# One x load divided into four transfers, so that the sixteen DMA engines carry unequal shares

## The chip, the cores and the metric

The kernel runs on one core of one Trainium2 chip. The metric is device microseconds of one execution, the median of several runs. The profile is one further execution, recorded by the hardware profiler; its span runs from the program's first instruction to its last.

## What is computed

Eight experts, each with its own 256 tokens, two weight matrices and two biases:

```
h = np.matmul(x, w1) + b1[:, np.newaxis, :]
h = np.maximum(h, 0)
return (np.matmul(h, w2) + b2[:, np.newaxis, :]).astype(np.float32)
```

x is 8 x 256 x 512, w1 is 8 x 512 x 2048, w2 is 8 x 2048 x 512, and the output is 8 x 256 x 512, all fp32 in HBM. The kernel computes in fp16 with fp32 sums.

## The kernel before

**Loads.** Every load that GpSimd issues (the queue that the profile calls q0) converts fp32 in HBM to fp16 in SBUF on the way. `load_w1` (L82 to L86) and `load_w2` (L88 to L93) move one expert's matrix, 128 partitions with 16 KB of fp16 each; the w2 of the last two experts goes in two halves of 8 KB a partition. `load_x` (L72 to L80) moves the x of several experts in one transfer: experts 2 and 3 together (tile x2, 128 partitions with 4 KB of fp16 each, which are 8 KB in HBM) and experts 4 to 7 together. In x2, partition p holds four consecutive tokens; expert 2 lies in partitions 0 to 63, expert 3 in 64 to 127. The x of experts 0 and 1 comes as fp32 through SyncE's queue (L194, q1 in the profile) and is converted by VectorE. In what follows, a row is one partition's share of such a transfer.

**Order on the GpSimd queue.** The order is written out by hand in `ring` (L218 to L228): w1 of expert 0, b2, w1 of expert 1, the x2 load (L76), w1 of expert 2; then, each put ahead of a stage and issued when a buffer comes free, w1 of 3, w2 of 0, x of 4 to 7, w1 of 4, w2 of 1, and so on to the two halves of the w2 of expert 7. Three buffers for w1 and three for w2 let several 2 MB transfers stand in the queue at a time. Behind all loads, the same queue carries two stores (`flush`, L138 to L140): the results of experts 0 to 3, and those of 4 and 5.

**Work on each expert.** VectorE transposes x in 32x32 blocks (`transposes`, L96 to L112). `first_product` (L114 to L135) does 64 matmuls of 128x256 with a relu on ScalarE, and `second_product` (L166 to L186) 2 bias matmuls and 32 matmuls of 128x512, three stages later (LAG = 3). The results leave PSUM through VectorE and ScalarE in `store` (L142 to L164).

**The last stores.** The results of expert 6 leave in three parts, which SyncE (q1) and ScalarE (q10) issue, and those of expert 7 in one of 128 rows, which SyncE issues (L163, L164). A row is 4 KB here. The parts are set in

```
PARTS = {E - 2: ((0, 25, False), (25, 121, True), (121, 128, False))}
```

that is 25 rows on q1, 96 rows on q10, and 7 rows on q1.

**Landing.** Each transfer ends with sixteen small writes of 4 bytes, one of each DMA engine, that count up its semaphore; the engine that consumes the data waits until all sixteen are there. GpSimd's transfers take eight semaphores in turn.

Of the kernel before, what the change touches and what calls it, by code (L numbers as in the profile page):

```python
# [10 lines left out]
def kernel(  # L11
# [9 lines left out]
    nc = tc.nc  # L21
# [4 lines left out]
    P = 128  # L26
# [13 lines left out]
    PARTS = {E - 2: ((0, 25, False), (25, 121, True), (121, 128, False))}  # L40
    nXF32 = 2
    X_LOADS = {2: 2, 4: 4}

    def ordered(ins):
        return tc.keep_in_program_order(ins)
# [26 lines left out]
    def load_x(first, n):  # L72

        R = n * T // P
        t = x_pool.tile([P, R, H], fp16, tag=f"x{first}", name=f"x{first}")
        ordered(nc.gpsimd.dma_start(  # L76
            out=t, in_=x[first : first + n].rearrange("e (p r) h -> (e p) r h", r=R)
        ))
        for i in range(n):
            x16[first + i] = (t, i * (P // n), R)  # L80

# [110 lines left out]
    for e in range(nXF32):  # L192
# [4 lines left out]
        out=b2_sb,  # L197
        in_=b2.rearrange("e h -> (e h)").rearrange("(o f) -> o f", o=1),
    ))

    for e in range(nXF32):
        t = x_pool.tile([P, nTB, H], fp16, tag=f"x{e}", name=f"x{e}")
# [6 lines left out]
    for b in range(nB):  # L209
        nc.vector.transpose(  # L210
            out=b1T[b * B : (b + 1) * B, nB - 1 - b : nB - 1 - b + nJ * B],
            in_=b1_rows.rearrange("r (i j) -> r j i", j=nJ),
# [5 lines left out]
    for s in range(1, E + LAG - 1):  # L218
        if s < E:
            if s in X_LOADS:  # L220
                ring.append((s - 2, load_x, (s, X_LOADS[s])))
            ring.append((s - 2, load_w1, (s,)))
        if s >= LAG:
            ring.append((s - 2, load_w2, (s - LAG,)))
# [43 lines left out]
```

## Time and profile before

| | us |
|---|---|
| time, median of 3 runs (lowest, highest) | 181.61 (181.37, 181.66) |
| span of the profiled execution | 179.7 |
| time outside the span (median less span) | 1.9 |
| TensorE matmul busy | 130.7 |
| VectorE busy | 87.4 |
| ScalarE busy | 71.0 |
| GpSimd busy | 12.5 |

| queue | what it carries | packets | MB |
|---|---|---|---|
| q0 | GpSimd's loads and two stores | 3200 | 38.28 |
| q1 | SyncE's x loads and last stores | 476 | 1.70 |
| q10 | ScalarE's b1 load and a last store | 160 | 0.46 |
| q8, q14 | instruction fetch | 8 | 0.12 |

How to read it: an engine's busy time counts its own instructions alone. For the DMA engines the profile keeps every packet's queue, start, duration and size, but not which of the sixteen engines moved it, nor from which transfer it is. In a view of a window, the packets that start within it are counted by queue, with their bytes (as written at the destination) and the time that they took as a share of sixteen engines over the window. Packets under 512 bytes are nearly all the 4-byte landing marks, so their count in a window tells how many engines have come to the end of a transfer there.

### The profile page before, as it was taken

To read this page: it belongs to the slowest core of one execution; us is meant where nothing else is said; L and a number is where in the kernel's file an instruction comes from. 1 tells how busy PE (TensorE), PEld (TensorE's weight loads), DVE (VectorE), ACT (ScalarE), POOL (GpSimd) and SP (SyncE) were. 2 spreads that over 40 slices of the span, in tenths; PEclk is the share of its full clock that TensorE was granted. 3 is DMA by queue.
4 is the path that set the end of the run, shared out by engine and by line. 5 is a ranking of instruction groups with operands and counts; after the bars stand their busy time and mean duration, and the time that the engine had idled before them with its cause. 6 is when DMAs were issued, how large, how long until landed. Compare 5 with 4: busy or idle time off the path is not lost.

```text
span 179.7 us, 1958 instructions
## 1 busy us (share of the span) xinstructions
PE 130.7 (73%) x784; PEld 87.4 (49%) x784; DVE 87.4 (49%) x125; ACT 71.0 (40%) x152; POOL 12.5 (7%) x27
## 2 busy tenths in 40 slices
PE   0005999159895970999769994959499986999960
PEld 0004899149793320794359543934189432434420
DVE  0999938990000199999998699203200020301010
ACT  3001699318793022491267406930559020020010
POOL 6000030200201010001100001000200021010000
PEclk9999999858999696599988999999969997899998
DMA  5999999999998999999999999999999999999995
GB/s 208 274 197 213 233 204 208 230 224 193 228 233 184 224 233 219 193 230 230 193 219 233 212 197 233 230 193 219 233 208 201 233 212 202 217 215 213 344 422 239
DMA packets 3844, 40.56 MB, mean 226 GB/s; under 512 B 460, under 2 KB 476, under 8 KB 1148
## 3 DMA queue, kind: packets, MB, share of 16 engines
q0 software_dynamic: 3200, 38.28, 96.4%
q1 hardware_dynamic: 476, 1.70, 2.5%
q10 hardware_dynamic: 160, 0.46, 0.6%
q8 instruction: 6, 0.10, 0.2%
q14 instruction: 2, 0.02, 0.0%
HBM read 71.39 MB, written 4.19 MB: 421 GB/s over the span
## 4 chain that ended last, share of the span: by engine, by line
DMA 67%; PE 27%; POOL 1%; issue 1%; ACT 0%; another core or an unknown queue 0%; POOLq 0%
DMA w1sb<-in_w_dram 44%; DMA w2sb<-in_w_dram 23%; PE po L178 17%; PE ph L121 10%; PE po L171 1%; POOL w1sb L84 1%; ACT out L157 0%; POOL b_sb L196 0%; POOL x L76 0%; POOLq L252 0%
## 5 line engine op out<-in xcount | busy, mean ns | idle before, releaser
L121 PE MATMUL ph<-xT,w1sb 128*128 128x256 f16 x512 | 66.7, 299 | 36.2 <-DMA w1sb<-in_w_dram 30.0
L121 PEld LDWEIGHTS <-w1sb 128*128 128x128 f16 x512 | 60.9, 148 | 42.7 <-DMA w1sb<-in_w_dram 38.6
L128 ACT ACTIVATE hT<-ph,b1T 128x256 f16<-128x256 f32 x128 | 56.7, 475 | 36.9 <-PE ph L121 22.1
L112 DVE STREAM_TRANSPOSE xT<-x 32x256 f16<-32x256 f16 (+1 forms) x64 | 52.7, 885 | 28.0 <-DMA x<-in_x_dram 22.0
L178 PE MATMUL po<-w2sb,hT 128*128 128x512 f16 x256 | 59.9, 395 | 6.6 <-DMA w2sb<-in_w_dram 6.5
L178 PEld LDWEIGHTS <-hT 128*128 128x128 f16 x256 | 25.7, 101 | 40.7 <-issue 14.4
L156 DVE COPY out<-po 32x512 f32<-32x512 f32 (+2 forms) x22 | 15.1, 688 | 52.5 <-PE po L178 52.2
L157 ACT COPY out<-po 32x512 f32<-32x512 f32 (+2 forms) x22 | 12.7, 578 | 65.5 <-PE po L178 65.3
L109 DVE STREAM_TRANSPOSE xT<-x 32x256 f16<-32x256 f16 x32 | 14.0, 436 | 0.5
L93 POOL DMA_DIRECT2D w2sb<-in_w_dram x10 | 5.3, 535 | 73.9 <-PE po L178 73.9
L84 POOL DMA_DIRECT2D w1sb<-in_w_dram x8 | 4.5, 559 | 62.7 <-PE ph L121 61.9
L171 PE MATMUL po<-b_sb,ones 1*128 1x512 f16 x16 | 4.8, 379 | 0.0
L210 DVE STREAM_TRANSPOSE b1T<-b_rows 32x512 f32<-32x512 f32 x4 | 4.1, 1028 | 0.0
L203 DVE CAST x<-x 128x1024 f16<-128x1024 f32 x2 | 1.4, 694 | 3.3 <-DMA x<-in_x_dram 3.3
L171 PEld LDWEIGHTS <-ones 1*128 1x128 f16 x16 | 0.9, 92 | 2.1 <-issue 2.1
L140 POOL DMA_DIRECT2D out_dram<-out x2 | 1.1, 540 | 11.1 <-ACT out L157 11.1
L189 ACT ACT_TABLE_LOAD x1 | 1.3, 1283 | 0.7 <-PEq L252 0.7
L76 POOL DMA_DIRECT2D x<-in_x_dram x2 | 1.1, 557 | 0.0
L188 DVE MEMSET ones<- 1x128 f16 x1 | 0.2, 165 | 0.8 <-PEq L252 0.8
L196 POOL DMA_DIRECT2D b_sb<-in_b_dram x1 | 0.5, 507 | 0.0
L189 ACT ACTIVATE warm<-ones 1x128 f16<-1x128 f16 x1 | 0.3, 308 | 0.0
L252 POOL MEMSET const-float32-0.0<- 128x1 f32 x1 | 0.1, 98 | 0.2 <-issue 0.2
(3 smaller groups left out, 0.3 us busy)
## 6 DMA issues: line engine op xcount, KB each, us to landing
w1sb<-in_w_dram POOLq DMA_DIRECT2D x8, 2048.0 KB, 37.0
w2sb<-in_w_dram POOLq DMA_DIRECT2D x6, 2048.0 KB, 49.7
w2sb<-in_w_dram POOLq DMA_DIRECT2D x4, 1024.0 KB, 24.0
out_dram<-out POOLq DMA_DIRECT2D x1, 2048.0 KB, 26.7
x<-in_x_dram SPq DMA_DIRECT2D x2, 512.0 KB, 4.0
x<-in_x_dram POOLq DMA_DIRECT2D x1, 1024.0 KB, 35.6
out_dram<-out POOLq DMA_DIRECT2D x1, 1024.0 KB, 17.7
x<-in_x_dram POOLq DMA_DIRECT2D x1, 512.0 KB, 24.5
```

What stands on the lines that cost most here:

```text
L84: ordered(nc.gpsimd.dma_start(out=w1_sb[e], in_=w1[e].rearrange("(p kc) m -> p kc m", kc=nKC)))
L93: ordered(nc.gpsimd.dma_start(out=w2_sb[e][:, lo : lo + half], in_=src[:, lo : lo + half]))
L109: nc.vector.transpose(out=out[:, :, g, :, 0, :], in_=block[:, :, :, 0, :])
L112: nc.vector.transpose(out=out[:, tb, g], in_=block[:, tb])
L121: ordered(nc.tensor.matmul(out=ph, lhsT=w1_sb[e][:, kc, :].rearrange("p (q j) -> p q j", j=nJ)[:, :, j], rhs=xT[e][:, kc, :], start=(kc == 0),
L128: nc.scalar.activation(out=hT[e][:, j, :].rearrange("p (tb k i) -> p tb k i", tb=nTB, k=split), in_=ph.rearrange("p (tb i k) -> p tb k i", ...
L156: nc.vector.tensor_copy(out=out_sb[at : at + rows, k * nTB, :], in_=po[0][part])
L157: nc.scalar.copy(out=out_sb[at : at + rows, k * nTB + 1, :], in_=po[1][part])
L171: ordered(nc.tensor.matmul(out=t, lhsT=ones1, rhs=b2_sb[0:1, e * H : (e + 1) * H], start=True, stop=False,))
L178: ordered(nc.tensor.matmul(out=po[tb], lhsT=hT[e][:, j, tb * P : (tb + 1) * P], rhs=w2_sb[e][:, j, :], start=False, stop=(j == nJ - 1),))
L189: ordered(nc.scalar.activation(out=warm, in_=ones1, func=mybir.ActivationFunctionType.Relu))
L210: nc.vector.transpose(out=b1T[b * B : (b + 1) * B, nB - 1 - b : nB - 1 - b + nJ * B], in_=b1_rows.rearrange("r (i j) -> r j i", j=nJ),)
```

## The change

The load of x2 is issued as four transfers in place of one: rows 0 to 79, 80 to 101, 102 to 126, and 127. The second and the third carry `max_dma_last_dim` = 4096, which cuts each row of 8 KB in HBM into two descriptors of 4 KB (22x2x1024 and 25x2x1024 elements); the last row is divided into 16 pieces of 128 elements without being told. By the words of the change, eleven DMA engines then carry 7 rows and five carry 10; before, each carried 8. The four stand where the one stood in GpSimd's order.

```diff
     X_LOADS = {2: 2, 4: 4}
+    SHARES = {2: ((0, 80, None), (80, 102, 4096), (102, 127, 4096), (127, 128, None))}
...
         t = x_pool.tile([P, R, H], fp16, tag=f"x{first}", name=f"x{first}")
-        ordered(nc.gpsimd.dma_start(
-            out=t, in_=x[first : first + n].rearrange("e (p r) h -> (e p) r h", r=R)
-        ))
+        src = x[first : first + n].rearrange("e (p r) h -> (e p) (r h)", r=R)
+        dst = t.rearrange("p r h -> p (r h)")
+        for p0, p1, cap in SHARES.get(first, ((0, P, None),)):
+            ordered(nc.gpsimd.dma_start(
+                out=dst[p0:p1], in_=src[p0:p1], **({} if cap is None else {"max_dma_last_dim": cap}),
+            ))
```

Other loads go through the same lines as one transfer of 128 rows, as before. On the other engines the instructions stay as they are, in their order. GpSimd has three instructions more. Since the semaphores are taken in turn, each later transfer of GpSimd has another one, and the waits of the engines follow: VectorE's first 16 transposes of x2 (expert 2) wait for the 80 rows alone, the next 8 for the 22 rows too, and the last 8 for the 25 rows and the single one.

## The prediction

> **What bounds the kernel now.** I read the page first, for the resource that is always busy:
>
> ```profile
> span 179.7 us, 1958 instructions
> ...
> DMA  5999999999998999999999999999999999999995
> ...
> q0 software_dynamic: 3200, 38.28, 96.4%
> ...
> q8 instruction: 6, 0.10, 0.2%
> ```
>
> The sixteen DMA engines are busy from the second slice to the last but one, nearly all with GpSimd's queue. Then the chain of work that ended last, its last 70 us:
>
> ```profile
> 108.47 41.12 DMA w2sb<-in_w_dram
> 149.59 0.04 issue
> 149.63 8.75 PE po L178 x32
> ...
> 166.47 7.03 PE po L178 x32
> ...
> 173.52 0.59 ACT out L157
> ```
>
> The last w2 load that TensorE waits for was issued 41 us before it landed: it stood in a queue that never runs dry. So no load is late because of its issue; a landing is late by what stands before it on the slowest of sixteen engines. The chain's last step is an ACT copy that ends at 174.11, and the span ends at 179.7. Between lie the last stores, on the same DMA engines. What the change can move is therefore each engine's sum of work, and the largest sum sets the end.
>
> Now the landings, by windows of the DMA view: first two windows at 46.0 to 46.9 and 46.9 to 48.0 (a load of w1), then 147.5 to 148.6 and 148.6 to 150.0 (the w2 load of the chain).
>
> ```profile
> DMA packets 31, 0.26 MB, mean 291 GB/s; under 512 B 15, under 2 KB 15, under 8 KB 15
> ...
> DMA packets 18, 0.27 MB, mean 246 GB/s; under 512 B 1, under 2 KB 1, under 8 KB 1
> ...
> DMA packets 30, 0.20 MB, mean 179 GB/s; under 512 B 11, under 2 KB 11, under 8 KB 11
> ...
> DMA packets 41, 0.29 MB, mean 211 GB/s; under 512 B 5, under 2 KB 5, under 8 KB 5
> ```
>
> Packets under 512 B are landing marks, one of each engine. Near 47 us one engine of sixteen is late, near 149 us five are, and each load waits for the late ones. What makes them late shows in the windows 28 to 160 and 30.4 to 30.6:
>
> ```profile
> q8 instruction: 5, 0.08, 0.2%
> ...
> q8 instruction: 1, 0.02, 27.9%
> ```
>
> By 160 us five instruction fetches have passed, and one of them took 27.9% of 16 x 0.2 us, 0.89 us, of one engine. Five fetches and five late engines: each fetch sets another engine back, for good, since the queue leaves no pause to make it up. The page counts a sixth.
>
> At the end of the span, windows 177.05 to 177.4, 177.4 to 177.9 and 177.9 to 178.5:
>
> ```profile
> DMA packets 37, 0.12 MB, mean 339 GB/s; under 512 B 8, under 2 KB 8, under 8 KB 37
> ...
> q1 hardware_dynamic: 34, 0.12, 83.1%
> q0 software_dynamic: 3, 0.00, 0.5%
> ...
> DMA packets 34, 0.14 MB, mean 279 GB/s; under 512 B 0, under 2 KB 0, under 8 KB 34
> ...
> q1 hardware_dynamic: 34, 0.14, 67.6%
> ...
> DMA packets 31, 0.08 MB, mean 137 GB/s; under 512 B 11, under 2 KB 11, under 8 KB 31
> ```
>
> The three q0 packets are marks of the earlier store, so 8 - 3 = 5 marks of the last store come by 177.4, none in the next half microsecond, and the other eleven after 177.9. Five engines are done 0.5 to 1.45 us before the other eleven. Six of the eleven are late by a fetch. The other five would be those of the 25-row store: in the window 170.2 to 170.8
>
> ```profile
> q1 hardware_dynamic: 5, 0.02, 8.3%
> ```
>
> q1 has five packets while q10 and q0 have more. Those five engines carry five rows of 25, where an even share would be less than two; a store row is 67.6% x 16 x 0.5 us / 34 = 0.159 us, so five are 0.8 us, as much as a fetch. Six and five give eleven only if they are different engines. So **eleven engines set the end and five have about a microsecond to spare.** That is the picture the change is to be put into.
>
> **The change part by part.** Prices come from four places: the x2 load in full stream (window 25.1 to 26.6), one mark (24.22 to 24.24), one mark with one 512-byte piece of b2 (14.49 to 14.51), and the rate of the 16 KB descriptors beside it (the row of 100 to 140).
>
> ```profile
> q0 software_dynamic: 79, 0.32, 106.7%
> ...
> q0 software_dynamic: 1, 0.00, 6.9%
> ...
> q0 software_dynamic: 2, 0.00, 25.3%
> ...
> 25.10:26.60 1.50, 1.50 (x16) 1.50 (x15) 0.00 (x0) 1.50 (x4) 1.00 (x2) 1.00 1.07 216
> ...
> 100.00:140.00 40.00, 32.24 (x202) 21.75 (x201) 15.58 (x16) 19.54 (x42) 1.58 (x3) 0.96 1.01 216
> ```
>
> - *A row of x2*: 79 rows in 1.5 us on 16 engines, 16 x 1.5 / 79 = **0.304 us**.
> - *A mark*: 6.9% x 16 x 0.02 us = **0.022 us**. Three transfers more are three marks more on each engine, 0.066 us.
> - *The single row in 16 pieces*: the two packets took 25.3% x 16 x 0.02 = 0.081 us, less the mark 0.059 us for 512 bytes. A piece of x2 is 256 bytes, so between 0.02 (its bytes at the row's rate) and 0.059 us; I take 0.03.
> - *A row in two descriptors*: not in this trace. One half costs between 0.152 us (half a row) and 0.304 us (as dear as a whole row). Descriptors four times as large as a row run at the same 216 GB/s, so a descriptor's own cost is hardly visible; I take 0.155. Ends for a cut row: 0.304 to 0.608 us, taken 0.31.
>
> Eleven engines: 5 whole rows and 2 cut ones, 1.52 + 0.62 + 0.066 + 0.03 = 2.24 us, where 8 rows and no extras were 2.43. **-0.2 us.** Five engines: 5 whole and 5 cut, 1.52 + 1.55 + 0.066 + 0.03 = 3.17 us, **+0.73 us.**
>
> If the five are those with time to spare, the end moves with the eleven: last marks from below 178.5 to below 178.3, and those of the five from 177.05 to 177.4 up to 177.8 to 178.1, still not last. The load of the chain goes the same way: its late five marks (last landing 149.59) come at 149.39, and the on-time ones that now carry 10 rows by 148.6 + 0.73 = 149.33. So TensorE's last stretch moves by the same 0.2 us.
>
> Now what the four issues do on the queues.
>
> ```profile
> 2.96 0.56 POOL L76 DMA_DIRECT2D x<-in_x_dram  x1
> 3.47 0.57 POOL L84 DMA_DIRECT2D w1sb<-in_w_dram  x1
> 25.60 0.53 POOL L84 DMA_DIRECT2D w1sb<-in_w_dram  x1 [21.56 <-PE ph L121]
> ...
> 26.64 0.56 POOL L76 DMA_DIRECT2D x<-in_x_dram  x1
> 32.59 0.54 POOL L84 DMA_DIRECT2D w1sb<-in_w_dram  x1 [5.39 <-PE ph L121]
> ...
> 27.54 12.85 DVE L112 STREAM_TRANSPOSE xT<-x 32x256 f16<-32x256 f16 x32 [3.38 <-PE ph L121]
> ...
> 38.09 8.84 PE L121 MATMUL ph<-xT,w1sb 128*128 128x256 f16 x64 [5.80 <-DMA w1sb<-in_w_dram]
> ```
>
> Three issues more at 0.56 us put the w1 load behind them from 3.47 to about 5.2 us. The engines reach x2 only near 24.2 us, and GpSimd issues nothing else until 25.60: the 1.7 us are hidden by 19 us of queued work. Without that cover they would cost 1.7 us once. The added waits on GpSimd (the semaphores are taken in turn, so a later load waits for an earlier one of its turn) fall on transfers that are long down: the x load of experts 4 to 7, at 26.64, waits for the second w1 load, whose marks pass in the window 24 to 25.1:
>
> ```profile
> DMA packets 56, 0.16 MB, mean 149 GB/s; under 512 B 16, under 2 KB 16, under 8 KB 56
> ```
>
> The w1 load at 32.59 waits for the 80 rows, and the w2 load queued behind it for the 22 rows, both down before 28.5. Nothing later comes nearer than that.
>
> VectorE transposes x2 from 27.54 on, 32 times 0.40 us. The first 16 need the 80 rows alone; the last 8 need the 25 rows, at worst 0.73 us later than now, and their turn is at 27.54 + 24 x 0.40 = 37.1 us. TensorE waits at 38.09 for w1, not for x. So nothing is late on this side; if the transposes did start 0.73 us later, the first half would end near 34.7, still 3 us ahead.
>
> **Sum:** the eleven engines' -0.2 us, against the profiled execution's own 179.7: 179.5. That execution lies 1.91 us below the median of the runs, 181.61, and the same outside part is added: **181.4 us**, 0.11% less. About 0.2% (0.36 us) is what a measurement of this kernel can tell from no change, so the likeliest case counts as "same". With the bounds of the marks and the cut rows it lies between 181.1 (no fees, and the chain gains a little beside) and 181.65 (cut rows each 0.1 us dearer).
>
> A rule of the Trainium skill speaks against the change: the page "DMA: Bandwidth & Descriptors", section "Rules for kernel authors", says not to divide a transfer by partitions, since the parts share the same engines and run one behind the other. Its section "Anatomy of one DMA — SWDGE (gpsimd) path" gives about 2 us fixed per transfer; three of those, by that figure, would make an estimated 187.6 us, a case like rival E below. The row of a mark (0.022 us) speaks for a far smaller price in a full queue.
>
> **The rivals.**
>
> *A. The five heavy engines are not the five with time to spare* (slower). The profile does not name engines, so it does not show that 25 rows land on the right ones. For the forecast: 22 rows on eleven and 25 on five cover all sixteen once, and every earlier GpSimd transfer has sixteen marks and an even number of rows for each engine, so a dealer that goes round has had no cause to leave its first engine; the 25-row store also takes one fixed block of five. Against it: nothing fixes that first engine. It decides with a single engine: if one heavy engine is among the eleven, that one ends 0.73 us later, 181.61 + 0.73 = 182.3 us.
>
> *B. The rows are dealt in another way* (the change doesn't do what it says; slower). If each transfer is dealt in shares of two rows from the first engine on, 22 rows go two to each of eleven engines, 25 two to each of twelve and one to a thirteenth. The first eleven then carry 5 + 2 + 2 = 9 rows, 1.52 + 4 x 0.31 + 0.1 = 2.86 us, +0.43: 182.0 us. The trace's 25-row store on five engines speaks against it, but that is another queue.
>
> On this the same page, section "Why a DMA increments its semaphore by 16 and not by 1", says that a transfer takes the largest number of engines up to 16 that divides its outermost size, so 11 for 22 and 5 for 25, from a cursor that goes round; this would be the forecast. It adds that some direct GpSimd copies get shares of the rounded-up size instead, which would be B. No run shown so far tells the two apart.
>
> *C. Cut rows are dear.* At the upper end, 0.304 us a half, a heavy engine has another 5 x 0.3 = 1.5 us: it ends at 177.4 + 0.73 + 1.5 = 179.6, 1.1 after the present end, 182.7 us. The even rate of small and large descriptors speaks against it.
>
> *D. The eleven don't set the end*, because the last store is tied to its issue, and that to TensorE's clock, which the throttle grants. Then 181.6. Against it:
>
> ```profile
> 166.58 7.91 SPq L164 DMA_DIRECT2D out_dram<-out  x3
> ```
>
> The last of these three is issued by 174.5; eight rows of 0.159 us are 1.3 us, yet the marks come 2.5 to 4 us later, behind queued rows.
>
> *E. Each further transfer pays its whole start*, unhidden. The nearest row is that of SyncE's x loads at the start, with nothing queued ahead (the last number is us from issue to landing):
>
> ```profile
> x<-in_x_dram SPq DMA_DIRECT2D x2, 512.0 KB, 4.0
> ```
>
> 4.0 us less 1.3 us for eight rows of 4 KB leave 2.7; three times that on top is 189.7 us. The row of a mark in the full queue speaks against it.
>
> **How the numbers follow.** Forecast 0.68, A 0.15, B 0.08, C 0.03, D 0.05, E 0.01. Within the forecast 0.14 of the whole chance lies beyond 0.36 us faster (engines that end together may also even out the waits between stages), 0.52 within, 0.02 slower by cut rows. Faster 0.14; same 0.52 + 0.05 = 0.57; slower 0.02 + 0.15 + 0.08 + 0.03 + 0.01 = 0.29. The likeliest case's own range is 181.1 to 181.65. To hold 8 in 10, the range must reach A: 181.1 to 182.35, which leaves out C, E and the tails.
>
> **What would show it.** In the profile of the changed kernel: 16 marks near 28 us spread over about 0.9 us, eleven first and five later; near 149 us ten late marks rather close together, all before 149.5; and in the last window of the span all sixteen marks of the last store within 0.6 us, the last about 0.2 us earlier. A would show as some engines ending alone, 0.7 us after the rest; B as nine rows' lateness near 27 us on eleven engines; C as packets of 2 KB that take over 0.2 us. The forecast falls if the end stays while the sixteen marks have drawn together, or if the five still end first.

## The result, and the profile after

The changed kernel takes 182.24 us (median of 7 runs, 182.02 to 182.50), where the kernel before takes 181.61 (7 runs, 181.37 to 181.90). The ratio is 1.0036, 95% interval 1.0024 to 1.0048: **slower by 0.36%**, 0.63 us. The forecast was 181.4 and "the same"; the time is that of rival A (182.3).

The page of the changed kernel, the lines on the DMA engines:

```profile
span 180.4 us, 1963 instructions
...
DMA packets 4084, 40.56 MB, mean 225 GB/s; under 512 B 654, under 2 KB 670, under 8 KB 1388
...
q0 software_dynamic: 3440, 38.28, 96.1%
```

The bytes are the same, in 240 packets more; the span is 0.7 us longer. The last 70 us of the chain of work that ended last have the same members as before, about 0.7 us later (lines left out are marked by dots):

```profile
109.28 41.02 DMA w2sb<-in_w_dram
150.30 0.04 issue
150.34 8.75 PE po L182 x32
...
174.23 0.59 ACT out L161
```

The landing moved from 149.59 to 150.30, and everything behind it went along. Why it landed later shows in the marks. First the first w1 load behind x2, windows 36.2 to 36.9, 37.4 to 37.6 and 38.5 to 38.7 of the changed kernel:

```profile
DMA packets 26, 0.25 MB, mean 351 GB/s; under 512 B 11, under 2 KB 11, under 8 KB 11
...
DMA packets 14, 0.16 MB, mean 819 GB/s; under 512 B 4, under 2 KB 4, under 8 KB 4
...
DMA packets 7, 0.10 MB, mean 492 GB/s; under 512 B 1, under 2 KB 1, under 8 KB 1
```

Eleven engines come first and five later, as the change says. But one of the five comes another 1.1 us later: the first instruction fetch, at 31.4 us, has hit one of the heavy engines, those with 10 rows. Then the end, windows 177.7 to 178.3, 178.3 to 179.1 and 179.1 to 179.3:

```profile
DMA packets 41, 0.11 MB, mean 184 GB/s; under 512 B 14, under 2 KB 14, under 8 KB 41
...
q1 hardware_dynamic: 39, 0.11, 45.8%
q0 software_dynamic: 2, 0.00, 0.2%
...
DMA packets 10, 0.04 MB, mean 51 GB/s; under 512 B 0, under 2 KB 0, under 8 KB 10
...
DMA packets 2, 0.00 MB, mean 0 GB/s; under 512 B 2, under 2 KB 2, under 8 KB 2
```

Two of the 14 marks are q0's. So twelve marks of the last store come together before 178.3, where the forecast wanted all sixteen; two had come before; and **two come alone, over 0.8 us behind the rest.** These two set the end. Before, the last marks fell below 178.5; now at 179.2, which is the 0.7 us of the span. The other late marks did move as the forecast had it, from below 178.5 to below 178.3.

### The profile page after: what moved, and what is told of

Read it like the earlier page. It is cut to its first block, busy times and chain, and to the rows that moved or that the text cites. A ratio compares the mean times of both kernels' runs of the same rounds, so it can differ in the third digit from the quotient of the medians.

```text
span 180.4 us, 1963 instructions
## 1 busy us (share of the span) xinstructions
PE 129.6 (72%) x784; PEld 86.7 (48%) x784; DVE 87.3 (48%) x125; ACT 70.9 (39%) x152; POOL 14.6 (8%) x30
## 4 chain that ended last, share of the span: by engine, by line
DMA 66%; PE 27%; POOL 2%; issue 1%; ACT 0%; another core or an unknown queue 0%; POOLq 0%
DMA w1sb<-in_w_dram 43%; DMA w2sb<-in_w_dram 23%; PE po L182 17%; PE ph L125 10%; POOL x L80 1%; PE po L175 1%; POOL w1sb L88 1%; ACT out L161 0%; POOL b_sb L200 0%; POOLq L256 0%
## 5 line engine op out<-in xcount | busy, mean ns | idle before, releaser
L125 PE MATMUL ph<-xT,w1sb 128*128 128x256 f16 x512 | 65.5, 295 | 37.9 <-DMA w1sb<-in_w_dram 31.8
L125 PEld LDWEIGHTS <-w1sb 128*128 128x128 f16 x512 | 60.2, 148 | 44.1 <-DMA w1sb<-in_w_dram 40.6
L132 ACT ACTIVATE hT<-ph,b1T 128x256 f16<-128x256 f32 x128 | 56.6, 475 | 37.6 <-PE ph L125 22.8
L80 POOL DMA_DIRECT2D x<-in_x_dram x5 | 3.1, 643 | 0.0
```

What stands on the lines that cost most here:

```text
L80: ordered(nc.gpsimd.dma_start(out=dst[p0:p1], in_=src[p0:p1], **({} if cap is None else {"max_dma_last_dim": cap}),))
L125: ordered(nc.tensor.matmul(out=ph, lhsT=w1_sb[e][:, kc, :].rearrange("p (q j) -> p q j", j=nJ)[:, :, j], rhs=xT[e][:, kc, :], start=(kc == 0),
L132: nc.scalar.activation(out=hT[e][:, j, :].rearrange("p (tb k i) -> p tb k i", tb=nTB, k=split), in_=ph.rearrange("p (tb i k) -> p tb k i", ...
```

## The experiments

Two theories stood at first. **P** (place): some of the heavy five are engines that are late anyway. **F** (fees): three further transfers with cut rows cost 0.6 us by themselves. All variants change the shares of the x2 load alone, unless another edit is shown. "Lone" marks are those that come well behind all others of their transfer, here of the last store unless another window is named; "the pack" is the large group that comes together before them; "ahead" are the few that come before the pack.

**Turned by two engines.**

```diff
-    SHARES = {2: ((0, 80, None), (80, 102, 4096), (102, 127, 4096), (127, 128, None))}
+    SHARES = {2: ((0, 64, None), (64, 66, 4096), (66, 88, 4096), (88, 113, 4096), (113, 127, 4096), (127, 128, None))}
```

> Six transfers: 64 rows, then 2, 22, 25 and 14 cut rows, then 1. If the dealer goes round from where it stands, the 2 rows turn it by two engines and the 14 bring it back, and the sums are again eleven engines with 7 rows and five with 10, but the five sit two engines further on. Theory P (place): in the changed kernel two of the heavy five were late engines and three had time to spare; turned by two in this direction all five have time to spare, the end moves by -0.1 us (one row less, five marks more): 181.5 us, all sixteen marks of the last store within 0.7 us and none alone. If it should be the other direction, four or five heavy engines end alone and the time stays near 182.3. Theory F (fees: each further transfer and its cut rows cost by themselves): 0.63 us for three further transfers make 1.05 for five, 182.7 us.

Measured: 182.28 us, ratio 1.0034 (1.0021 to 1.0047). F's 182.7 is wrong: two transfers more cost nothing that shows. P's first branch is wrong too; turning did not help. Its second branch, four or five marks alone and a time near 182.3, fits in both numbers. The end of its profile, windows 177.65 to 178.5 and 178.9 to 179.5:

```profile
DMA packets 48, 0.16 MB, mean 183 GB/s; under 512 B 12, under 2 KB 12, under 8 KB 46
...
q0 software_dynamic: 6, 0.02, 4.8%
...
DMA packets 10, 0.02 MB, mean 41 GB/s; under 512 B 4, under 2 KB 4, under 8 KB 10
```

The six q0 packets make 0.02 MB, two 8 KB rows and four marks. That leaves eight marks in the pack, four lone ones, and four ahead. The place matters, as P says: another place, another number of lone marks, but the same time.

**The 25 rows first.**

```diff
+    SHARES = {2: ((0, 80, None), (80, 105, 4096), (105, 127, 4096), (127, 128, None))}
```

> The 25 rows ahead of the 22, all else as in the changed kernel. P: the heavy five sit on five other engines, those next in the round; some of them are late engines, and one is enough, so 182.2 to 182.4 us; the number of marks that come alone, about 0.9 us after the rest, is another than two (three, if the late engines lie next to each other as theory P has them). F: 182.24 us and no reason for another number of lone marks.

Measured: 182.33 us, ratio 1.0032 (1.0021 to 1.0044). Windows 177.9 to 178.3 and 178.7 to 179.3:

```profile
DMA packets 25, 0.07 MB, mean 174 GB/s; under 512 B 8, under 2 KB 8, under 8 KB 25
...
q0 software_dynamic: 2, 0.00, 0.3%
...
DMA packets 11, 0.02 MB, mean 41 GB/s; under 512 B 5, under 2 KB 5, under 8 KB 11
```

Six in the pack, five alone, five ahead: the cleanest of the patterns, though P had wanted three alone. It reads best so: the six are the engines with a fetch; the five alone are heavy and late for another reason, the 25-row store. (Five heavy engines that a fetch has hit would give the same counts; the run with an even store below speaks against it, since there the same load leaves none alone.) So with the 25 rows first, the heavy five are the very five of that store, engines 0 to 4 in the store's own count, and the dealer starts at the first engine. With the 22 rows first, the heavy five are then 11 to 15. This is where the forecast wanted them, and still two were late.

**Four transfers in even shares.**

```diff
+    SHARES = {2: ((0, 80, None), (80, 96, 4096), (96, 112, 4096), (112, 128, None))}
```

> Four transfers of 80, 16, 16 and 16 rows, two of them with cut rows: each engine carries 8 rows as before, with three further transfers. P: only the fees are left, three marks and two cut rows, +0.07 us: 181.7 us, with eleven late marks and five early ones at the end as before. F: as in the changed kernel, 182.1 to 182.3 us.

Measured: 181.62 us, ratio 1.0004 (0.9993 to 1.0016), beside 181.65 of the kernel before. F is refuted: without uneven shares, three further transfers and cut rows cost nothing that can be measured; the interval allows 0.3 us at most, and F asks for about 0.5 or more.

**The same shares without cutting.**

```diff
+    SHARES = {2: ((0, 80, None), (80, 102, None), (102, 127, None), (127, 128, None))}
```

> The changed kernel's 80, 22, 25 and 1 rows without cutting a row. If 22 and 25 rows are dealt as the cut ones were, the marks of the x load come as eleven and, 0.9 us later, five, and the time is 182.2 us, a trifle less for the uncut rows. If they are dealt in shares of two from the first engine on, eleven engines carry 9 rows: 182.0 us, with no group of five late marks near 28 us, and at the end as many late marks as before.

Measured: 181.90 us, ratio 1.0014 (1.0004 to 1.0023). The first w1 load behind x2, windows 35.7 to 36.6 and 36.7 to 38.2:

```profile
DMA packets 18, 0.21 MB, mean 237 GB/s; under 512 B 5, under 2 KB 5, under 8 KB 5
...
DMA packets 36, 0.41 MB, mean 273 GB/s; under 512 B 11, under 2 KB 11, under 8 KB 11
```

Here five engines are early and eleven late, the reverse of the cut version: the eleven with 9 rows, and five with 7, 6, 5, 5 and 5. Uncut rows are dealt in shares of two from the first engine on. Rival B's mechanism exists, at a little less than its price (0.25 us, where 0.43 was reckoned), but the cut takes this load out of its reach. At the end, window 178.2 to 179.4, nine marks are late, where as many as before, eleven, were expected:

```profile
DMA packets 29, 0.08 MB, mean 68 GB/s; under 512 B 9, under 2 KB 9, under 8 KB 29
```

So what makes two of 11 to 15 late? The six fetches. Two readings were set against each other: **X**, they sit on fixed engines; **M**, they move from one execution to the next.

**Turned the other way.**

```diff
+    SHARES = {2: ((0, 64, None), (64, 78, 4096), (78, 100, 4096), (100, 125, 4096), (125, 127, 4096), (127, 128, None))}
```

> As the turned variant, but turned two engines the other way (64 rows, then 14, 22, 25 and 2 cut rows, then 1), so that the heavy five sit on engines 9 to 13, counted from the first engine of the store's five as 0. Two readings of the profiles so far. M (the instruction fetches move: each execution goes on round the eleven engines 5 to 15 from where the last one stopped, six engines a time): there is a late engine among the five in 9 or 10 of 11 executions, whichever five of 5 to 15 are taken, so 182.2 to 182.4 us again, and the number of lone marks at the end is any from 0 to 5. X (the fetches sit on fixed engines, 14, 15 and 5 to 8, as the changed kernel's profile alone would have it): 9 to 13 are just the ones with time to spare, all sixteen marks at the end within 0.8 us, 181.5 us.

Measured: 182.07 us, ratio 1.0026 (1.0016 to 1.0035): slower, so X's 181.5 is wrong. Windows 177.7 to 178.3 and 178.8 to 179.1:

```profile
DMA packets 43, 0.13 MB, mean 212 GB/s; under 512 B 12, under 2 KB 12, under 8 KB 43
...
q0 software_dynamic: 2, 0.00, 0.2%
...
DMA packets 5, 0.01 MB, mean 27 GB/s; under 512 B 3, under 2 KB 3, under 8 KB 5
```

Ten in the pack, three alone, three ahead. X, with none alone, is wrong in its engines too.

**The heavy five on engines 0 to 4, with an even store; and the even store alone.** For the first, the 25 rows come first as above, and the store is changed; for the second, the kernel before has the change of the store alone.

```diff
-    PARTS = {E - 2: ((0, 25, False), (25, 121, True), (121, 128, False))}
+    PARTS = {E - 2: ((0, 16, False), (16, 112, True), (112, 128, False))}
```

> The heavy five on the engines 0 to 4 (the 25 rows ahead of the 22), and the results of expert 6 stored in even shares (16, 96 and 16 rows: eight rows an engine), so that the five have no more store rows than the others. M: the fetches never come to 0 to 4, so the five heavy ones are always those with time to spare: against the even store with the undivided load 0.2 us less, 181.7 us, eleven marks together at the end and five before them. X: the same, 181.7 us.

> The kernel before, with the results of expert 6 stored in even shares (16, 96 and 16 rows). The reference for the run with the heavy five on engines 0 to 4. Both readings: the six engines with a fetch have two store rows more than before, 2 x 0.16 us: 181.9 us; at the end six marks late by about 0.9 us, ten early.

Measured: 181.57 us with the heavy five (ratio to the kernel before 1.0003, 0.9994 to 1.0012) and 181.76 without (1.0005, 0.9996 to 1.0014). The difference of 0.19 us is what was expected, but the intervals overlap, and that of the even store alone, for which 0.3 us was foreseen, includes no cost at all; by time these runs don't decide. The ends of the profiles say more. With the heavy five, window 178.0 to 178.5; without, 178.2 to 178.9:

```profile
DMA packets 25, 0.06 MB, mean 115 GB/s; under 512 B 11, under 2 KB 11, under 8 KB 25
```

```profile
DMA packets 16, 0.04 MB, mean 53 GB/s; under 512 B 7, under 2 KB 7, under 8 KB 16
```

With the heavy five, eleven marks end together by 178.5 and none is alone; without, seven late marks, where six were expected, reach to 178.9. So heavy engines that no fetch hits do not end alone, and in these two executions the end came earlier with the uneven shares. That this gains the 0.2 us reckoned is not shown: it is one execution of each. The version is no faster than the kernel before, which does the same through its store.

**The changed kernel again, twice.**

> The changed kernel itself, one more execution in profile. M: the first fetch hits another engine than in the first profile, and the number of lone marks at the end is any from 0 to 5, with the number of marks ahead of the rest the same. X: again two lone marks, two early ones, and the first two fetches on heavy engines.

> The changed kernel a third time in profile. M: lone marks of any number from 0 to 5, by fetches whose place in the order of six need not be that of either profile before; 182.2 us with at least one lone mark, 181.4 us with none. X: two lone marks from the first two fetches.

Measured: 182.10 and 182.00 us (one execution each), two lone marks both times. Now the order of the fetches. The window 57.2 to 58.2 holds the last marks of a w2 load after two fetches. First the first profile of the changed kernel, then the second, then the third:

```profile
DMA packets 27, 0.20 MB, mean 205 GB/s; under 512 B 2, under 2 KB 2, under 8 KB 2
```

```profile
DMA packets 23, 0.19 MB, mean 188 GB/s; under 512 B 0, under 2 KB 0, under 8 KB 0
```

```profile
DMA packets 25, 0.20 MB, mean 205 GB/s; under 512 B 0, under 2 KB 0, under 8 KB 0
```

In the first profile, the first two fetches have hit heavy engines by then; in the other two, none has. The second profile's lone marks come from its last two fetches: in its window 140.0 to 140.5, after five fetches, one mark is alone, and in 164.4 to 164.8, after all six, two are (both windows of the third profile have the same counts):

```profile
DMA packets 6, 0.08 MB, mean 164 GB/s; under 512 B 1, under 2 KB 1, under 8 KB 1
```

```profile
DMA packets 13, 0.09 MB, mean 225 GB/s; under 512 B 2, under 2 KB 2, under 8 KB 2
```

The same program, the same shares, first two fetches on heavy engines and then four on light ones, or four on light and then two on heavy: X is refuted as it stands. But marks alone would also fit the same six engines in another order. The fetches themselves say more. Each is one packet of 16 KB, and what it takes, as the share of sixteen engines over 0.2 us (27.9% are 0.89 us, 30.4% are 0.97), repeats from profile to profile:

| profile | the six fetches of q8 in order of time, % |
|---|---|
| changed kernel, second and third | 27.9, 27.9, 29.7, 29.5, 29.2, 30.4 |
| changed kernel, first | 30.4, 30.0, 27.9, 27.9, 29.6, 29.5 |
| the 25 rows first | 29.2, 30.5, 30.4, 30.1, 27.9, 27.9 |
| four even shares | 29.6, 29.5, 29.2, 30.5, 30.5, 30.0 |

These are pieces of one round of eight: 27.9, 27.9, 29.6, 29.5, 29.2, 30.4, 30.4, 30.0. The thirteen profiles all fit it, seven begun at its first place, four at the seventh, one each at the third and the fifth. The duration goes with the place in the round and not with the number of the fetch. So a place in the round stands for something that stays the same, most simply a DMA engine, and in the changed kernel's first profile other places were hit than in the second: the fetches move. M's round holds in kind, with eight places where M had eleven engines.

**A staircase, twice.** To read the engines off, each of the engines 15 down to 8 gets its own number of rows.

```diff
+    SHARES = {2: ((0, 29, None), (29, 54, None), (54, 75, None), (75, 92, None), (92, 112, None), (112, 128, None))}
```

> The x load of experts 2 and 3 as a staircase: six uncut transfers of 29, 25, 21, 17, 20 and 16 rows, dealt in shares of ceil(rows/16) from the first engine on, so that the engines 15 down to 8 carry 1, 2, 3, 4, 5, 6, 9 and 10 rows and 0 to 7 carry 11. Afterwards every landing shows its marks as stairs of 0.3 us (0.9 between engines 10 and 9), and an engine that a fetch hits leaves its stair by 0.9 us: the fetches' engines can be read off. M: six different engines, none of them 0 to 4; X: 14, 15 and four of the eight with 11 rows. The three rows more on the first eight engines, some with a fetch or the extra store rows, make it slow: 181.6 + 0.9 + 0.1 = 182.6 us.

> The staircase again, the same program in another execution. M: again six different engines, not 0 to 4, but not the same six as in the run before, or the same in another order. X: the same six in the same order. 182.6 us by both.

Measured: 182.54 and 182.75 us (one execution each), as expected for a slow arrangement. The windows of the first staircase: 78.4 to 80.0 (a w2 load after two fetches) and 160.8 to 162.3 (one after all six), each over the stairs 15 to 10; 79.9 to 81.0 and 89.6 to 90.7, each over stair 9, before and after the third fetch; then 107.4 to 108.9 and 146.1 to 147.2, over the stairs 15 to 10 again, after four and five fetches:

```profile
DMA packets 28, 0.36 MB, mean 225 GB/s; under 512 B 6, under 2 KB 6, under 8 KB 6
...
DMA packets 41, 0.31 MB, mean 208 GB/s; under 512 B 3, under 2 KB 3, under 8 KB 3
...
DMA packets 15, 0.23 MB, mean 209 GB/s; under 512 B 1, under 2 KB 1, under 8 KB 1
...
DMA packets 14, 0.23 MB, mean 209 GB/s; under 512 B 0, under 2 KB 0, under 8 KB 0
...
DMA packets 23, 0.29 MB, mean 197 GB/s; under 512 B 5, under 2 KB 5, under 8 KB 5
...
DMA packets 22, 0.25 MB, mean 223 GB/s; under 512 B 4, under 2 KB 4, under 8 KB 4
```

After two fetches all six stairs from 15 to 10 are in place, and so is 9: the first two went to engines with 11 rows. The third took engine 9 off its stair, and by the end three of 10 to 15 are off. They go in turn, 10, 11, 12, each with one of the last three fetches. Engine 8 keeps its stair throughout. X's engines, 14 and 15 among them, are refuted here too. The second staircase shows the same counts in the first four windows; M's "not the same six, or in another order" was not seen in this pair. Both staircases began at the first place of the round, so its third to sixth places are the engines 9, 10, 11 and 12. That fits the second profile of the changed kernel, which began there too: its fifth and sixth fetches, on 11 and 12, are the ones that left a mark alone.

## Why the prediction was wrong, point by point

- **What bounds the kernel: right.** The largest sum among sixteen engines sets the end, eleven are late and five have time to spare. In every variant the time follows the last marks, whichever engine they are of.
- **The prices: right.** A heavy engine was to be 0.73 us later; with the last marks at 179.2 in place of 178.5, it is 0.7. The engines with fewer rows were to be 0.2 us earlier; the pack ends below 178.3 in place of 178.5 (one execution of each). The fees were put at 0.1 us; the even shares show 181.62 beside 181.65, within the noise. Rivals C (dear cut rows) and E (whole starts), and the estimate of 187.6 us, fall with that. Rival D falls too: the last of SyncE's three stores was issued 0.7 us later (by 167.29 + 7.91 = 175.2 us), and the pack ended earlier all the same:

```profile
167.29 7.91 SPq L168 DMA_DIRECT2D out_dram<-out  x3
```

- **GpSimd, VectorE, the added waits: right.** The four issues stand in the chain with 2.56 us in one piece, and the w1 load behind them still lands 33 us after its issue. It lands at 38.87 (TensorE went on behind it at 38.09 before), and it is a single mark, the one near 38.6, that makes it later: of the others, eleven come from 36.2 to 36.9, where the kernel before has fifteen, so the delay of the issue is covered. VectorE begins to transpose x2 earlier, at 26.66 in place of 27.54, since it waits for the 80 rows alone; that its row names PE is the profile's choice among several semaphores. The chain's two pieces, and the row of VectorE:

```profile
2.97 2.56 POOL x L80 x4
5.53 33.34 DMA w1sb<-in_w_dram
```

```profile
26.66 12.85 DVE L116 STREAM_TRANSPOSE xT<-x 32x256 f16<-32x256 f16 x32 [2.53 <-PE ph L125]
```

- **The dealing: right for this load.** Eleven engines carry 7 rows and five 10. The Trainium skill, page "DMA: Bandwidth & Descriptors", section "Why a DMA increments its semaphore by 16 and not by 1", has both ways of dealing; the runs agree with both, the one for cut rows (eleven marks early, five late), the other for uncut ones (five early, eleven late).
- **"If the five are those with time to spare": here it failed.** The argument for it was about the dealer, that it stands at its first engine. That held: the 25 rows first fall on the store's five, so behind the 22 they fall on 11 to 15. But the argument said nothing of where the fetches go; it took the five engines without a fetch and without extra store rows to be a block at the end of the sixteen. They are not, as the two lone marks show (0.7 us on the span), and they are not the same in each execution. The views gave only a count, six and five, and a count was read as a place.
- **Rival A** had mechanism, price and deciding point: one heavy engine among the late ones is enough. Two, four, five and three lone marks gave 182.24, 182.28, 182.33 and 182.07. It got 0.15 where it should have had most of the chance: of the eleven engines outside the store's five, six are hit by a fetch, and five heavy ones miss them all only if the two sets fit exactly.

One reading fits the counts of all ten profiles with uneven shares or stairs: the round of eight lies on the engines 5, 6 and 9 to 14, in this order, and six of them are hit in an execution. Wherever it begins, engines 11 to 15 hold two or more of the six, so no execution spares the heavy five. The uncut load, begun at the first place, is a test: its eleven engines with 9 rows are 0 to 10, of these 0 to 4 have the store and 5, 6, 9 and 10 a fetch, which makes the nine late marks seen. The staircases show 9 to 12 in turn and 8 left out. That 7 and 15 are left out is inferred from the numbers of lone and early marks and not shown by itself: 7 could stand in place of 5 or 6, and 15 in place of 14. What the beginning hangs on stays open. The four that were seen, first, seventh, fifth and third, lie six places apart, as if each execution went on where another had stopped, but no run shows two executions in a row.

No arrangement was found that beats the kernel before. By the prices above there is little left, as an estimate: a lighter load for thirteen engines against 7, 8 and 15 would give about half a row, 0.15 us, and its transfers cost 0.1.

## What to carry to other kernels

Where queues never run dry, count the work of each DMA engine, and ask for every engine that is to carry more whether something else also lands on it; what the program does not issue itself, such as instruction fetches, counts too. A pattern of late and early marks says how many engines are late, not which; give the engines different shares in a probe and read them off before tuning by place. Uneven shares are only worth placing where the other load is fixed by the program: the five engines of the 25-row store are so, those without a fetch are not. And where a count of marks fits two readings, look for something in the trace that tells the members apart, as the durations of the fetches did here.

## What the runs showed of the hardware that was not expected

- A transfer dealt to some of the engines also sends small packets to the others. The page counts 654 packets under 512 bytes, where that of the kernel before counts 460, so 194 more: 48 are the marks of three transfers and 16 the pieces of the single row. The other 130 are as many as 5 engines x 4 descriptors (of the 22-row transfer, in which five engines have no share) and 11 x 10 (of the 25-row one). The same count, one packet for each descriptor that an engine has less than the fullest one, gives 162 for the turned load, 17 for the uncut one and 48 for the staircase, and the pages' 718, 541 and 588 leave just these. What the packets are for is not shown.
- Whether a row is cut in two decides how its transfer is dealt: 25 rows go five each to five engines when cut, and two each to twelve and one to a thirteenth when not.
- The instruction fetches of one program fell on other DMA engines in another execution: near 57 us two lone marks in one profile of the changed kernel, none in two others. Their durations, 0.89 to 0.97 us, repeat in a round of eight, of which an execution takes six.
